# A decoder trunk on one core: the low parts of the down-projection weights made by accumulating DMA transfers

## The chip, the core and the metric

The kernel runs on 1 core of one Trainium2 chip. A time is the device time of one execution in microseconds. The time before is 1220.44 us, the median of 2 runs (1219.15 to 1221.73).

## What is computed

A two-layer decoder trunk on 256 tokens of width 1024 (float32, batch 1). Each layer adds to the residual h: half a SwiGLU feed-forward, a mixer (a state-space group beside a differential attention group, joined by one output projection), a cross attention into 256 memory tokens, and half a second SwiGLU. A final RMS norm follows.

```python
def swiglu(x, w_gate, w_up, w_down):
    return (jax.nn.silu(x @ w_gate) * (x @ w_up)) @ w_down
...
for l in range(DEPTH):                      # DEPTH = 2, D_MODEL = 1024, D_FF = 2816
    h = h + 0.5 * swiglu(rms_norm(h, ffn1_norm[l]), ffn1_w_gate[l], ffn1_w_up[l], ffn1_w_down[l])
    h = h + hybrid_mixer(rms_norm(h, mix_norm[l]), ...)
    h = h + memory_cross_attention(rms_norm(h, xattn_norm[l]), rms_norm(mem, mem_norm[l]), ...)
    h = h + 0.5 * swiglu(rms_norm(h, ffn2_norm[l]), ffn2_w_gate[l], ffn2_w_up[l], ffn2_w_down[l])
return rms_norm(h, final_norm)
```

There are four feed-forwards, and so four down projections of 2816 x 1024.

## The kernel before, in words

**Split products.** A matrix product is made of three products in the type float32r. Each operand is split into a high part, its copy in float32r, and a low part, what is left of it. The product is high x high + high x low + low x high. In the profile a weight's parts are called whi and wlo, an activation's xh and xl (or gT, oT, yT for both parts).

**The weight stream.** All weights lie in memory as 384 units of 128 x 1024 numbers (512 KB), in the order of their use (`stream_plan`, line 72). A unit is loaded by SyncE into one of 4 raw buffers (`load_to`, lines 450 to 453; N_RAW, line 33) and split in two halves of 512 columns into one of 5 pairs of hi and lo buffers (`split_unit`, line 457; N_W, line 34). ScalarE copies raw to hi, VectorE subtracts hi from raw into lo (`split`, line 408). For weights that follow a norm, the gain is multiplied in by both. A unit costs TensorE 12 matmuls of 512 columns, since there are two token tiles of 128, two halves and three products.

**Feed-forward** (`ffn`, line 707). 11 chunks of 256 hidden columns each take 4 units of the gate and up weights. ScalarE's silu (tile sg) and VectorE's product with the up half (tile g) follow, then transposes into gT. Two chunks behind, 2 units of the down projection are accumulated for each chunk (`mm_b`, line 513). So a steady period holds 6 units: 4 of gate and up, 2 of down. After the last chunk the last 4 down units remain. `blocks` (line 616) runs them all over the first token tile and then all over the second, so that the tail work of the first tile can begin early. During that first pass a new unit is wanted after only 6 matmuls. Each feed-forward has 22 down units, 18 in nine pairs and 4 in the tail.

**What sets the order.** The program is laid out in Python, instruction by instruction, by an estimated clock (`Clock`, line 122). Chains such as silu and transposes, the norm statistics, or the tables of the state-space model are tasks that are given out between the products of the main stream. Each engine then works through its own list in that order, and semaphores hold it wherever its data aren't there. Before each group of three products `tick` (line 493) calls `feed` (line 431), which gives out every half unit that is due: one wanted at most LEAD = 4.0 estimated us after the present place of the main stream, and only if its buffers are among the next 5 units. Units are given out strictly in order, so a down unit comes after the gate and up units ahead of it. `unit` (line 479) forces the unit that is wanted now.

**Buffers.** A raw buffer is loaded anew when all readers of it are done: ScalarE's copy and VectorE's subtraction of both halves. A hi or lo buffer is written anew when TensorE is done with the unit five before.

**Lines in the profile.** Helpers record every operation of an engine at one line: VectorE L223, ScalarE L257, GpSimd L280, matmuls L296, transposes L307, weight loads of the stream L453.

Of the kernel before, what the change touches and what calls it, by code (L numbers as in the profile page):

```python
# [11 lines left out]
F32 = mybir.dt.float32  # L12
# [3 lines left out]
AF = mybir.ActivationFunctionType  # L16
ALU = mybir.AluOpType
# [16 lines left out]
N_W = 5  # L34
N_S4 = 12
N_T5 = 3
LEAD = 4.0
STEP = 1.28
MARGIN = 0.2
BURST = 0.8  # L40
# [29 lines left out]


def stream_plan():
    """units of the weight stream in the order of use: (matrix, layer, index, kind, gain, units taken tile by tile)"""
    plan = []
    for l in range(L):
        def ffn(nm):
            for j in range(NCH):
                for kp in range(4):
                    plan.append((nm + "_gu", l, 4 * j + kp, "A", (nm, l, 2 * kp), 4 if j == 0 and len(plan) >= 4 else 1))
                if j >= LAG:  # L80
                    for f in range(2):
                        plan.append((nm + "_dn", l, 2 * (j - LAG) + f, "B", None, 1))
            for n in range(2 * (NCH - LAG), 2 * NCH):
                plan.append((nm + "_dn", l, n, "B", None, 2 * LAG))

        def chunk(nm, c, norm, skew):
            for kp in range(4):
                plan.append((nm, l, 4 * c + kp, "A", (norm, l, 2 * kp), skew))

        ffn("ffn1")  # L90
        for c in range(4):
            chunk("w_in", c, "mix", 4 if c == 0 else 1)
        for c in range(3):
            chunk("wkv", c, "mem", 1)
        for k in range(4):
            plan.append(("w_glu", l, k, "B", None, 4))
        for k in (4, 5, 6, 7, 0, 1, 2, 3):
            plan.append(("w_out", l, k, "B", ("ssm", l, k) if k < 4 else ("sub", l, 0), 4))
        for c in range(2):
            chunk("wq", c, "xattn", 4 if c == 0 else 1)  # L100
        chunk("wkv", 3, "mem", 1)
        for k in range(8):
            plan.append(("wo", l, k, "B", None, 4))
        ffn("ffn2")
    need, at, i = [], 0.0, 0
    while i < len(plan):
        n = plan[i][5]
        need += [at + STEP * k for k in range(n)]
        at += 2 * STEP * n
        i += n  # L110
    return plan, need


class Task:
    """a chain of instructions that is emitted piece by piece between the products of the main stream"""

    def __init__(self, gen, now):
        self.gen, self.t, self.done, self.waiters = gen, now, False, []
# [1 line left out]


class Clock:
    """Orders the emission: an estimate of when each engine gets to what it has been given."""

    def __init__(self, nc):
        self.nc = nc
# [38 lines left out]

    @contextmanager
    def aside(self):
        """what is given out here does not hold up the chain"""
        t = self.cur.t
        yield  # L170
        self.cur.t = t
# [11 lines left out]
                self.resume(x)  # L183

    def step_idle(self):
        """nothing to give the tensor engine: on to the next chain"""
        wake, _, x = heapq.heappop(self.heap)
        self.now = max(self.now, wake)
        self.resume(x)
# [122 lines left out]
class Trunk:  # L312
# [29 lines left out]
        self.mmfree = [0.0, 0.0]  # L342
        self.tpfree, self.tpown = [0.0, 0.0], {}

# [1 line left out]
    def s4t(self, shape, dt=F32, name="s4"):  # L346
        return self.s4.tile(shape, dt, tag="s4", name=name)

# [13 lines left out]
        self.tpfree[self.tpown.pop(id(p))[1]] = self.c.cur.t  # L362

    def tp_wait(self):
        """inside a task: until a bank for transposes is free"""
        while self.tpfree[-2] + TPW > self.c.now:
            yield max(self.c.now + 0.01, min(self.tpfree[-2] + TPW, self.c.now + 0.3))

# [20 lines left out]
        self.mmfree.append(self.c.cur.t)  # L389

    def acc_wait(self):
        """inside a task: until an accumulator is free"""
        while self.nacc >= 2 or self.accfree[0] + ACCW > self.c.now:
            yield self.c.now + 0.25 if self.nacc >= 2 else self.accfree[0] + ACCW

# [5 lines left out]
    def xt(self):  # L401
        return [self.xp.tile([128, 8, 128], F32R, tag=k, name=k) for k in ("xh", "xl")]

# [1 line left out]
    def copy(self, out, in_, scale=1.0):  # L405
        self.a.activation(out, in_, AF.Copy, scale=scale)

# [16 lines left out]
        return p  # L424

    def fork(self, *gens):
        """run chains side by side inside a task"""
        return [self.c.spawn(g, self.c.cur.t) for g in gens]

# [1 line left out]
    def feed(self, least=-1):  # L431
        """give out the halves of the units that are due, at least those of unit `least`"""
        c = self.c
        prev, c.cur = c.cur, self.stream
        n = len(self.plan)
        while self.nsplit < 2 * n:
            u, q = divmod(self.nsplit, 2)
            if u >= self.nfree + N_W or (u > least and self.need[u] + q * STEP / 2 > self.main + LEAD):
                break
            self.split_next()  # L440
        c.cur = prev
# [15 lines left out]
    def split_unit(self, i, q):  # L457
        kind, gain = self.plan[i][3:5]
        if q == 0:
            hi = self.hip.tile([128, 1024], F32R, tag="hi", name="whi")  # L460
            lo = self.lop.tile([128, 1024], F32R, tag="lo", name="wlo")
            self.w[i] = [hi, lo, 0.0, 0.0]
        hi, lo = self.w[i][:2]
        s = slice(512 * q, 512 * q + 512)
        r = self.raw[i]
        self.stream.t = 0.0
        if gain is None:
            self.split(hi[:, s], lo[:, s], r[:, s])
        else:
            nm, l, k = gain  # L470
            g = l * NGAIN + GOFF[nm] + k + (q if kind == "A" else 0)
            gc = self.gains[:, g:g + 1]
            self.a.activation(hi[:, s], r[:, s], AF.Copy, scale=gc)
            self.v.scalar_tensor_tensor(lo[:, s], r[:, s], gc, hi[:, s].bitcast(F32), op0=ALU.mult, op1=ALU.subtract)
        self.w[i][2 + q] = self.stream.t
        if q == 1:
            del self.raw[i]
# [11 lines left out]
    def free_unit(self):  # L489
        self.nfree += 1  # L490

# [1 line left out]
    def tick(self, ready):  # L493
        self.feed()
        self.c.run_due()
# [23 lines left out]
                self.p.matmul(acc[n], a, b[:, s], start=first and p == 0, stop=last and p == 2)  # L519

    def project(self, name, x, evac, preps=None):
        """a chunk of 512 columns for both token tiles; evac(t, psum) is the chain that follows"""
        self.c.run_due()
        ps = [self.mmt(), self.mmt()]
        out = []
        if preps is not None:
            us = []
            for t in range(2):
                self.c.wait(preps[t])
                for k in range(4):  # L530
                    if t == 0:
                        us.append(self.unit(name))
                    self.mm_a(ps[t], x[t], us[k], 2 * k, k == 0, k == 3)
                    if t == 1:
                        self.free_unit()
                out.append(self.c.spawn(evac(t, ps[t])))
        else:
            for k in range(4):
                u = self.unit(name)
                for t in range(2):  # L540
                    self.mm_a(ps[t], x[t], u, 2 * k, k == 0, k == 3)
                    if k == 3:
                        out.append(self.c.spawn(evac(t, ps[t])))
                self.free_unit()
        self.c.run_due()
        return out

    def opening(self, evac):
        """the first chunk, while x and the weights are still on their way in"""
        c = self.c  # L550
        c.now = c.busy["act"] = c.busy["dve"] = 3.9
        ps = [self.mmt(), self.mmt()]
# [53 lines left out]
        out = []  # L606
# [7 lines left out]
        return out  # L614

    def blocks(self, name, accs, xs, n, first, last, tail=None):
        """n units over token tile 0, then over tile 1; xs(t, k) is the stationary pair"""
        us = []
        out = []
        end = self.upos + n == len(self.plan)  # L620
# [9 lines left out]
                out.append(self.c.spawn(tail(t, accs[t])))  # L630
        return out

# [1 line left out]
    def prep(self, t, acc, coef):  # L634
        h = self.h[t]
        t0 = []
# [66 lines left out]
        return  # L703
        yield

# [1 line left out]
    def ffn(self, nm, preps, tail):  # L707
        bank = {}
        gT = {}
# [54 lines left out]
        base = NCH - LAG  # L764
        return self.blocks(nm + "_dn", accs, lambda t, k: xs(base + k // 2, k % 2, t), 2 * LAG, False, True, tail)

# [1 line left out]
    def exp_acc(self, out, x, n):  # L768
        v = self.v
        k, r, q = (self.sp1.tile([128, n], F32, tag=f"e{i}{n}", name="ex") for i in "krq")  # L770
# [20 lines left out]
        self.v.tensor_scalar(out, out, -MAGIC, None, op0=ALU.add)  # L791
        yield

# [1 line left out]
    def ssm_tables(self, l, tb):  # L795
        v, a, g, io = self.v, self.a, self.g, self.io
        t16 = lambda nm: self.sp1.tile([128, 16], F32, tag="p_" + nm, name=nm)
# [177 lines left out]
                g.dma_start(tt[r0:r0 + 16, :, j:4, :], ks[64 * e:64 * e + 16, :, 0:4 - j, :])  # L975
            yield

# [1 line left out]
    def mixer(self, l, preps, tb, tables, tail):  # L979
        v, c = self.v, self.c  # L980
        vt = w = cs = dtt = None
# [112 lines left out]
        def ssm_out(states):  # L1094
# [29 lines left out]
            for pb in range(2):  # L1124
                yield from self.tp_wait()
                p = self.transpose4(ygf, [256 * i + 128 * pb for i in range(4)])
                # columns of p are (i, gh, c): channel block 2*gh+pb, token 4*c+i
                pv = p.rearrange("p (i g c) -> p i g c", i=4, g=2)
                o = [x.rearrange("p (g b) (c i) -> p b i g c", b=2, i=4)[:, pb] for x in yt]
                self.split(o[0], o[1], pv)  # L1130
                self.tp_done(p)
# [156 lines left out]
        c.wait(*go)  # L1288
        return self.blocks("w_out", accs, lambda t, k: (mx[t][0][:, k, :], mx[t][1][:, k, :]), 4, False, True, tail)

# [1 line left out]
    def val_evac(self, ch, tag, after):  # L1292
        def f(t, ps):
            for x in after:
# [119 lines left out]
                    self.free_unit()  # L1414
        return self.blocks("wo", accs, lambda t, k: xs(t, 4 + k), 4, False, True, tail)

# [1 line left out]
    def setup(self):  # L1418
        nc, io, c = self.tc.nc, self.io, self.const
        g = self.g  # L1420
# [131 lines left out]


def lay_out(a):
    """host side: permutations, repeats and joins of the inputs"""
    f = {k: np.asarray(v) for k, v in a.items()}

    def type_a(w):
# [53 lines left out]
```

## Time and profile before

| | |
|---|---|
| median of 2 runs | 1220.44 us |
| span of the profiled execution, first to last instruction | 1217.4 us |
| TensorE's granted clock | 0.999 |
| VectorE, subtractions raw - hi without a gain (wlo<-raw,whi) | 224, mean 686 ns |
| ScalarE, copies raw to hi without a gain (whi<-raw) | 224, mean 624 ns |
| weight loads from memory on SyncE's queue | 382 of 512 KB, median 4.2 us to landing |
| read from memory | 207.06 MB |

Of the 224 halves without a gain 176 belong to the down projections (88 units); the other 48 are those of the gated linear unit and of the cross attention's output. The own time of the profiled execution is not listed apart from its span; the two runs of the table lie 1.8 to 4.3 us above that span. In the group lines the name left of the arrow is what is written, the names right of it are what is read; after the count stand the busy time, the mean of one in ns, and the idle time of the engine just before such instructions with what ended it. In a timeline a row gives the start, the time taken, engine, line and operation, and how many were merged. A stretch's row gives the length, then busy time and count for TensorE, its weight loads, VectorE, ScalarE and GpSimd, then the granted clock, the DMA engines' busy share and GB/s.

### The profile page before, as it was taken

What the parts mean: (1) busy time and instruction counts of PE and PEld (TensorE: products, weight loads), DVE (VectorE), ACT (ScalarE), POOL (GpSimd) and SP (SyncE); (2) the same over time, 40 slices, a digit from 0 to 9 for tenths busy, and PEclk for the clock granted to TensorE, in tenths of its full rate; (3) what the DMA queues carried; (4) which work ended last, traced back from release to release, by engine and by line L of the source; (5) the groups of instructions that cost most, each with busy time, mean ns of one, the idle gap of its engine ahead of it and who ended that gap; (6) DMA issues with size and microseconds to landing.
All of it is one profiled execution on the core that took longest, in us unless ns stands there. A gap on an engine that the chain in (4) does not pass through costs nothing.

```text
span 1217.4 us, 17907 instructions
## 1 busy us (share of the span) xinstructions
PE 1202.3 (99%) x6622; PEld 979.5 (80%) x6622; DVE 833.0 (68%) x1505; ACT 702.7 (58%) x1277; POOL 48.9 (4%) x111
## 2 busy tenths in 40 slices
PE   9999999999999999999999999999999999999997
PEld 7878888777888888888888888887678888888886
DVE  5787776498866678777666555565978675655664
ACT  6664545557857565644565544555686665644553
POOL 2110001000100010000100000000000000000000
PEclk9999999999999999999999999999999999999999
DMA  8566556534544466645656555655446445555652
GB/s 288 184 189 211 158 171 184 174 121 139 188 159 139 143 200 189 193 150 183 174 183 203 169 182 191 207 164 149 137 126 206 153 139 173 186 192 192 207 175 85
DMA packets 60439, 211.76 MB, mean 174 GB/s; under 512 B 7301, under 2 KB 8677, under 8 KB 60352
## 3 DMA queue, kind: packets, MB, share of 16 engines
q1 hardware_dynamic: 56448, 203.06, 52.6%
q0 software_dynamic: 2320, 6.08, 1.7%
q10 hardware_dynamic: 1584, 1.49, 0.4%
q8 instruction: 52, 0.85, 0.3%
q14 instruction: 35, 0.29, 0.1%
HBM read 207.06 MB, written 1.84 MB: 172 GB/s over the span
## 4 chain that ended last, share of the span: by engine, by line
PE 93%; DVE 2%; DMA 1%; ACT 1%; issue 1%; ACTq 0%; POOLq 0%; POOL 0%; DVEq 0%
PE mm L296 54%; PE acc L296 32%; PE tp L307 5%; PE tp L296 2%; DMA uq<-z 1%; DVE wlo L223 1%; DVE p L223 1%; ACT whi L257 0%; DVE nm L223 0%; DMA h<-in_x 0%; ACT z L257 0%; ACT junk L257 0%; ACT up L257 0%; ACTq L266 0%; DVE sb L223 0%
## 5 line engine op out<-in xcount | busy, mean ns | idle before, releaser
L223 DVE SCALAR_TENSOR_TENSOR wlo<-raw,gains,whi 128x512 fp32r<-128x512 f32 x544 | 383.4, 746 | 96.1 <-ACT whi L257 91.8
L257 ACT ACTIVATE whi<-raw,gains 128x512 fp32r<-128x512 f32 x544 | 353.4, 713 | 14.2 <-DMA raw<-in_wst 6.8
L296 PE MATMUL mm<-whi,xh 128*128 128x512 f32 x896 | 357.0, 398 | 0.0
L296 PE MATMUL mm<-whi,xl 128*128 128x512 f32 x896 | 349.8, 390 | 0.0
L296 PE MATMUL mm<-wlo,xh 128*128 128x512 f32 x896 | 349.5, 390 | 0.3 <-DVE wlo L223 0.3
L296 PE MATMUL acc<-whi,gT 128*128 128x512 f32 x704 | 240.0, 402 | 0.0
L296 PEld LDWEIGHTS mm<-whi,xh 128*128 128x128 f32 x896 | 168.5, 188 | 37.4 <-issue 2.4
L296 PEld LDWEIGHTS mm<-whi,xl 128*128 128x128 f32 x896 | 168.5, 188 | 35.8
L296 PEld LDWEIGHTS mm<-wlo,xh 128*128 128x128 f32 x896 | 168.8, 188 | 32.8 <-DVE wlo L223 0.6
L223 DVE TENSOR_TENSOR wlo<-raw,whi 128x512 fp32r<-128x512 f32 x224 | 147.3, 686 | 36.1 <-ACT whi L257 34.4
L257 ACT ACTIVATE whi<-raw 128x512 fp32r<-128x512 f32 x224 | 130.6, 624 | 62.2 <-DMA raw<-in_wst 41.0
L257 ACT ACTIVATE sg<-mm,rstd 128x256 f32<-128x256 f32 x88 | 41.8, 475 | 194.7 <-PE mm L296 194.5
L296 PEld LDWEIGHTS acc<-whi,gT 128*128 128x128 f32 x704 | 132.2, 188 | 26.8 <-issue 1.1
L296 PE MATMUL acc<-wlo,gT 128*128 128x512 f32 x352 | 137.4, 390 | 0.0
L223 DVE SCALAR_TENSOR_TENSOR g<-mm,rstd,sg 128x256 f32<-128x256 f32 x88 | 42.4, 482 | 127.1 <-ACT sg L257 126.5
L296 PE MATMUL mm<-whi,mem 128*128 128x512 f32 x256 | 92.6, 410 | 0.0
L296 PEld LDWEIGHTS acc<-wlo,gT 128*128 128x128 f32 x352 | 66.4, 189 | 11.0
L257 ACT ACTIVATE xh<-tp 128x512 fp32r<-128x512 f32 x40 | 23.9, 598 | 76.9 <-PE tp L307 76.9
L296 PEld LDWEIGHTS mm<-whi,mem 128*128 128x128 f32 x256 | 48.1, 188 | 11.5 <-issue 1.3
L296 PE MATMUL mm<-wlo,mem 128*128 128x512 f32 x128 | 50.9, 398 | 3.5 <-DVE wlo L223 3.5
L223 DVE TENSOR_TENSOR xl<-tp,xh 128x512 fp32r<-128x512 f32 x40 | 27.5, 687 | 31.4 <-ACT xh L257 31.4
L223 DVE TENSOR_TENSOR gT<-tp,gT 128x512 fp32r<-128x512 f32 x44 | 30.4, 691 | 26.7 <-ACT gT L257 26.6
(218 smaller groups left out, 1099.8 us busy)
## 6 DMA issues: line engine op xcount, KB each, us to landing
raw<-in_wst SPq DMA_DIRECT2D x382, 512.0 KB, 4.2
h<-in_x SPq DMA_DIRECT2D x4, 256.0 KB, 5.3
raw<-in_wst SPq DMA_DIRECT2D x4, 256.0 KB, 5.3
mem<-in_mem POOLq DMA_DIRECT2D x2, 512.0 KB, 6.7
uq<-z ACTq DMA_DIRECT2D x8, 128.0 KB, 4.7
bglu<-in_b_glu POOLq DMA_DIRECT2D x2, 512.0 KB, 4.0
scr<-sk POOLq DMA_DIRECT2D x4, 192.0 KB, 3.4
out_h<-fo SPq DMA_DIRECT2D x2, 320.0 KB, 2.3
```

Source lines behind the costliest of these rows:

```text
L223: r = getattr(self.e, name)(*a, **k)
L257: r = self.e.activation(out, in_, func, **k)
L296: r = self.e.matmul(out, lhsT, rhs, **k)
L307: r = self.e.transpose(out, in_, ident)
```

## The change

Units of the down projections (names that end in `_dn`) are split in another way. ScalarE copies raw to hi as before, and then copies hi, negated, to lo. After the second half one DMA transfer issued by GpSimd adds the whole unit of weights onto lo, 128 x 1024 numbers, so that lo holds weights minus hi. For units of odd number its source is the raw buffer, for those of even number the weights in memory once more. Both halves count as ready, in the estimated clock, when this transfer is. `feed` gives such units out up to DMA_LEAD = 3.0 us earlier. VectorE no longer takes part in these units.

```diff
 LEAD = 4.0
+DMA_LEAD = 3.0
...
-            if u >= self.nfree + N_W or (u > least and self.need[u] + q * STEP / 2 > self.main + LEAD):
+            early = DMA_LEAD if self.plan[u][0].endswith("_dn") else 0.0
+            if u >= self.nfree + N_W or (u > least and self.need[u] + q * STEP / 2 > self.main + LEAD + early):
                 break
...
-        if gain is None:
+        if self.plan[i][0].endswith("_dn"):
+            self.a.activation(hi[:, s], r[:, s], AF.Copy)
+            self.a.activation(lo[:, s], hi[:, s].bitcast(F32), AF.Copy, scale=-1.0)
+            if q == 1:
+                self.g.dma_start(lo, r if i % 2 else self.io["wst"][i], accum_op=ALU.add)
+                self.w[i][2] = self.stream.t
+        elif gain is None:
             self.split(hi[:, s], lo[:, s], r[:, s])
```

The rest of the diff takes out comments and docstrings.

## The prediction

> **What bounds the kernel now.** I read first the page's busy times and its chain of waits, then the table of who waited for whom, then busy times by stretch. The four stretches are the steady parts of the four feed-forwards, in order; the fifth is one period of six weight units.
>
> ```profile
> span 1217.4 us, 17907 instructions
> PE 1202.3 (99%) x6622; PEld 979.5 (80%) x6622; DVE 833.0 (68%) x1505; ACT 702.7 (58%) x1277; POOL 48.9 (4%) x111
> PE 93%; DVE 2%; DMA 1%; ACT 1%; issue 1%; ACTq 0%; POOLq 0%; POOL 0%; DVEq 0%
> ```
>
> ```profile
> PEld mm L296 <- DVE wlo L223: 6.7, 7, 1.8
> PE mm L296 <- DVE wlo L223: 3.8, 5, 1.4
> ...
> L296 PE MATMUL acc<-wlo,gT 128*128 128x512 f32 x352 | 137.4, 390 | 0.0
> L296 PE MATMUL mm<-wlo,mem 128*128 128x512 f32 x128 | 50.9, 398 | 3.5 <-DVE wlo L223 3.5
> ```
>
> ```profile
> 37.00:198.00 161.00, 161.00 (x936) 128.84 (x935) 125.20 (x296) 85.57 (x150) 12.95 (x25) 1.00 0.61 184
> 434.00:610.00 176.00, 176.00 (x1009) 143.40 (x1008) 131.74 (x288) 96.47 (x168) 8.83 (x18) 1.00 0.59 180
> 650.00:820.00 170.00, 170.00 (x776) 140.13 (x775) 99.82 (x155) 89.30 (x156) 1.49 (x4) 1.00 0.57 187
> 1040.00:1194.00 154.00, 154.00 (x698) 126.75 (x697) 89.36 (x139) 80.02 (x139) 0.00 (x0) 1.00 0.57 188
> ...
> 1160.00:1176.80 16.80, 16.80 (x77) 13.85 (x76) 9.73 (x16) 8.74 (x16) 0.00 (x0) 1.00 0.56 189
> ```
>
> TensorE is busy in every microsecond of all four feed-forwards, at a granted clock of 1.00. The matmuls that read a down projection's low part (acc<-wlo,gT) never stood idle: 0.0 us before 352 of them. What TensorE does wait on VectorE's low parts (3.8 and 6.7 us, which overlap) falls elsewhere: the idle row is that of the memory projections (mm<-wlo,mem), which the change leaves alone. So VectorE's work on the down projections costs nothing now, and taking it away can't make these stretches shorter. The question is only whether the new way delivers late.
>
> **The change, part by part.** Removed and added on the engines:
>
> ```profile
> L223 DVE TENSOR_TENSOR wlo<-raw,whi 128x512 fp32r<-128x512 f32 x224 | 147.3, 686 | 36.1 <-ACT whi L257 34.4
> L257 ACT ACTIVATE whi<-raw 128x512 fp32r<-128x512 f32 x224 | 130.6, 624 | 62.2 <-DMA raw<-in_wst 41.0
> ...
> L280 POOL DMA_DIRECT2D mem<-in_mem x2 | 1.2, 594 | 0.0
> ```
>
> There are 4 x 22 = 88 down units of two halves. VectorE loses 176 subtractions of 686 ns, 121 us: worth 0, as shown. ScalarE gains 176 copies; with no such row I price them as its plain half copies, 624 ns: 110 us. In one period that is 4 x 0.62 = 2.5 us on top of 8.74 of 16.80, so ScalarE still has 5.6 us over, and the cost by volume is 0. Without that cover it would be 2.5 us in each of 36 periods, 90 us. GpSimd issues 88 transfers, at about 0.6 us each (the mem row) 53 us on an engine busy for 48.9; what queues behind a waiting issue there is the two-step rstd, of which a feed-forward needs two, ahead of its first unit. I take 0 for that. Even units read their weights a second time from memory, 44 x 0.524 = 23 MB beside 203 MB.
>
> What does count is latency. The low part was ready one VectorE instruction after the high part. Now it is ready after four ScalarE copies and a whole 512 KB accumulating transfer, issued only after the second half. Call d the time from the last copy to the landing. No accumulate is in the trace; the nearest rows are plain transfers:
>
> ```profile
> raw<-in_wst SPq DMA_DIRECT2D x382, 512.0 KB, 4.2
> mem<-in_mem POOLq DMA_DIRECT2D x2, 512.0 KB, 6.7
> bglu<-in_b_glu POOLq DMA_DIRECT2D x2, 512.0 KB, 4.0
> scr<-sk POOLq DMA_DIRECT2D x4, 192.0 KB, 3.4
> bias<-scr POOLq DMA_DIRECT2D x1, 512.0 KB, 5.3
> fn<-in_final_norm POOLq DMA_DIRECT2D x1, 512.0 KB, 5.1
> ```
>
> GpSimd's 512 KB transfers land in 4.0 to 6.7 us. One pass of a unit through the 16 engines takes 0.56 x 16.80 / 6 = 1.6 us. An accumulate must read its target as well as its source. Low end: the second reading is free, d = 0.6 + 4.0 = 4.6. High end: the slowest row and a whole extra pass, d = 0.6 + 6.7 + 1.6, rounded to 9.0. I take the middle, 6.8, because loads of weights run beside it in every period, as beside the slow mem row.
>
> The Trainium skill bears on the second reading (Collectives: The Full Stack, "Part 3: Why 7× under link rate — side-by-side accounting"): an add in the DMA engine needs two source reads on one ring, and a reduce there came out at half the rate of a copy (measured ratio 1.93). By it a unit's accumulate would take an estimated 1.93 x 1.6 = 3.0 us of all engines; without it 1.6, and d would stand about 1.5 us apart between the two. No accumulate in this trace tells which.
>
> Now the time that is there. The code gives down units out up to 3 us earlier, so that the second unit's second half no longer stands behind a silu; but transfers can't start before the weights, slots and ScalarE allow. A steady pair of down units in the last feed-forward:
>
> ```profile
> 1150.63 1.15 ACT L257 ACTIVATE whi<-raw 128x512 fp32r<-128x512 f32 x2 [0.95 <-DMA raw<-in_wst]
> 1152.50 0.63 ACT L257 ACTIVATE whi<-raw 128x512 fp32r<-128x512 f32 x1 [0.72 <-DMA raw<-in_wst]
> ...
> 1160.03 0.40 PE L296 MATMUL acc<-wlo,gT 128*128 128x512 f32 x1
> ...
> 1163.02 0.39 PE L296 MATMUL acc<-wlo,gT 128*128 128x512 f32 x1
> ```
>
> First unit: 1150.63 + 2.5 = 1153.1, wanted at 1160.03: 6.9 us for the transfer. Second: copies end at 1155.6, wanted at 1163.02: 7.4. With d = 6.8 nothing is late; with 9.0 it is 2.1 a pair.
>
> In the first layer's feed-forwards (936 and 1009 TensorE instructions of the first two stretches against 776 and 698 of the others: the state-space tables are made between the products) some pairs have less:
>
> ```profile
> 187.40 1.66 ACT L257 ACTIVATE whi<-raw 128x512 fp32r<-128x512 f32 x3
> ...
> 195.06 0.40 PE L296 MATMUL acc<-wlo,gT 128*128 128x512 f32 x1
> ...
> 584.10 1.66 ACT L257 ACTIVATE whi<-raw 128x512 fp32r<-128x512 f32 x3
> ...
> 589.59 0.39 PE L296 MATMUL acc<-wlo,gT 128*128 128x512 f32 x1
> ```
>
> These leave 195.06 - 189.9 = 5.2 and 589.59 - 586.6 = 3.0 us, 4.1 in the mean. I choose 9 of the 36 pairs as such, half of those of that layer. With d = 6.8 each is 2.7 late: 24 us.
>
> The four tails are the worst place. There the last four down units are run over one token tile first, so that a unit is wanted each 1.36 us, while ScalarE now needs 2.5 for one:
>
> ```profile
> 1184.25 1.15 ACT L257 ACTIVATE whi<-raw 128x512 fp32r<-128x512 f32 x2 [0.94 <-DMA raw<-in_wst]
> ...
> 1193.41 0.48 ACT L257 ACTIVATE sg<-mm,rstd 128x256 f32<-128x256 f32 x1 [0.37 <-PE mm L296]
> ...
> 1195.25 0.60 ACT L257 ACTIVATE gT<-tp 128x512 fp32r<-128x512 f32 x1 [0.84 <-PE tp L307]
> 1195.74 3.74 ACT L257 ACTIVATE whi<-raw 128x512 fp32r<-128x512 f32 x7
> ...
> 1203.45 0.39 PE L296 MATMUL acc<-wlo,gT 128*128 128x512 f32 x1
> ```
>
> After the second sg (1193.9) stand half of the second tail unit (1.25), gT (to 1195.9), its other half (to 1197.1) and the third (to 1199.6). The fourth also needs its raw buffer: it is that of the second unit before the tail, which an accumulate now reads until it lands. That unit's copies end at 1184.25 + 2 x 2.5 = 1189.25, it lands at 1196.05, and the new load (4.2) at 1200.25. So the fourth is copied by 1202.75 and lands at 1209.55, where it was wanted at 1203.45: 6.1 late, four times, 24 us.
>
> Sum with d = 6.8: 0 + 24 + 24 = 48 us. The profiled execution's span is 1217.4 us; the runs' median, 1220.44, has 3.0 more around it, which I leave as it is: 1220.4 + 48 = 1268.5 us. With d = 4.6: 0 + 9 x 0.5 + 4 x 3.25 (ScalarE alone holds the tail, 1199.6 + 2.5 + 4.6 against 1203.45) = 17.5, 1238 us. With d = 9.0: 27 x 2.1 + 9 x 4.9 + 4 x 10.5 = 143, 1363 us.
>
> **The rivals.** *The lead covers it.* If the second reading rides along and the landing is like scr's 3.4, d is 4.0: no pair is late, and a tail only by 1199.6 + 2.5 + 4.0 - 1203.45 = 2.65. That is 11 us, 1231 us, not to be told from no change. It decides wherever d is below 5.1 (9 x 1.0 + 4 x 3.75 = 24 us, 2%). For it: bglu's 4.0 and the 7 us of a steady pair. Against: mem's 6.7, fn and bias above 5. The Trainium skill's fit for transfers issued by GpSimd (DMA: Bandwidth & Descriptors, "Anatomy of one DMA") gives an estimated 2.0 + 524 KB / 436 = 3.2 us for a plain one; every 512 KB row here is above it.
>
> *The DMA engines become the bound.* A period's loads take 0.56 x 16.80 = 9.4 us of them. Two accumulates fit as long as each takes under (16.80 - 9.4) / 2 = 3.7 us, 2.3 passes. At four passes, 6.4 us each, a period lasts 22.2, 5.4 more: 36 x 5.4 = 194, and a tail's four accumulates with four loads 32 us against some 17, 4 x 15 = 60: 1475 us. For it: the traffic is already 0.57 to 0.61. Against: no row here shows so slow a transfer.
>
> *The relief helps.* If the waits on low parts went, TensorE would gain at most 6.7 us, 1214 us. Against: they aren't where down units are split, and the accumulate is no shortcut even if all goes as meant.
>
> **How the numbers follow.** Late by a few microseconds in tails and short pairs (1268.5): 0.48. Covered (1231): 0.29. DMA-bound, or d at 9 and above: 0.21. Relief: 0.02, half of it over 2%. A measurement of this kernel can tell about 2% from no change. The range, 1227 to 1365, runs from a little under the covered case to d = 9.0 and leaves out most of the DMA-bound one. Slower by over 2%: 0.48 + 0.21 and little of the rest, 0.69; within 2%: 0.30; faster: 0.01.
>
> **What would show it.** VectorE's wlo<-raw,whi falls from x224 to x48; ScalarE shows x176 copies of whi into wlo near 620 ns; GpSimd 44 + 44 transfers into wlo. Right: these land in 5 to 7 us after issue, TensorE's acc<-wlo,gT has some 48 us of idle time that a DMA into wlo ended, half of it in four places, and the second layer's steady pairs show none. Wrong: that idle time lies evenly over all 36 pairs, or the DMA share nears 1 in the periods (then the engines are the bound), or TensorE stays busy through the tails (then the lead covers it).

## The result, and the profile after

The changed kernel takes 1364.34 us (median of 2 runs, 1364.12 to 1364.57) where the kernel before takes 1220.44: a ratio of 1.119, 95% interval 1.117 to 1.121, 144 us slower. Forecast were 48 us. The page of the changed kernel, first its span, busy times and chain, then groups:

```profile
span 1362.3 us, 18270 instructions
PE 1250.9 (92%) x6622; PEld 1004.4 (74%) x6622; DVE 725.6 (53%) x1329; ACT 813.3 (60%) x1453; POOL 125.5 (9%) x199
PE 57%; DMA 22%; issue 13%; ACT 4%; DVE 4%; ACTq 0%; POOLq 0%; POOL 0%; DVEq 0%; SPq 0%
...
L297 PE MATMUL acc<-whi,gT 128*128 128x512 f32 x704 | 263.7, 438 | 0.5 <-ACT gT L258 0.5
L297 PE MATMUL acc<-wlo,gT 128*128 128x512 f32 x352 | 155.6, 442 | 96.0 <-DMA wlo<-in_wst 65.9
...
L258 ACT ACTIVATE wlo<-whi 128x512 fp32r<-128x512 f32 x176 | 111.4, 633 | 5.6
...
L281 POOL DMA_DIRECT2D wlo<-in_wst x44 | 38.4, 874 | 575.8 <-ACT wlo L258 428.7
```

Two things lengthened the span by 144.9 us. TensorE idles 1362.3 - 1250.9 = 111.4 us where it idled 15.1, 96.3 more, and 96.0 of idle time stands before the products with a down unit's low part, the row that had 0.0. And TensorE is busy for 1250.9 us with the same 6622 instructions that took 1202.3, 48.6 more: the two acc rows above rose from 402 and 390 ns a product to 438 and 442. The DMA rows:

```profile
q1 hardware_dynamic: 56448, 203.06, 46.8%
q0 software_dynamic: 14992, 52.22, 20.0%
...
raw<-in_wst SPq DMA_DIRECT2D x382, 512.0 KB, 4.5
wlo<-in_wst POOLq DMA_DIRECT2D x44, 512.0 KB, 7.7
wlo<-raw POOLq DMA_DIRECT2D x44, 512.0 KB, 7.7
```

An accumulate lands 7.7 us after its issue, from either source. GpSimd begins to issue 0.29 us after the last copy's end (median over the 72 units of the pairs), so the forecast's d is 8.0, not 6.8. A steady pair, in TensorE's timeline:

```profile
1232.67 0.48 PE L297 MATMUL acc<-whi,gT 128*128 128x512 f32 x1
1234.43 0.47 PE L297 MATMUL acc<-wlo,gT 128*128 128x512 f32 x1 [1.28 <-DMA wlo<-in_wst]
```

Nearly every pair waits, 33 of the 36, not only the short ones: the first low part of a pair is used, at the median, 0.13 us after its landing. From the first down unit to the start of the tail the second layer's feed-forwards last 20.5 and 19.2 us longer than before, the first layer's 28.2 and 33.0. The tails are 11.2, 9.3, 13.6 and 10.4 longer. That is 101 us in the pairs and 45 in the tails. Of these, 66 and 30 are idle time before low parts; the rest is the busier TensorE.

The last tail shows the second loss. After the long wait the products stand 0.42 us apart, and then 0.23 again; the stretches' rows give the granted clock (the column after GpSimd's):

```profile
1341.25 0.63 PE L297 MATMUL acc<-whi,gT 128*128 128x512 f32 x2
1345.75 0.79 PE L297 MATMUL acc<-wlo,gT 128*128 128x512 f32 x1 [3.88 <-DMA wlo<-raw]
1346.35 1.05 PE L297 MATMUL acc<-whi,gT 128*128 128x512 f32 x2
1347.20 0.63 PE L297 MATMUL acc<-wlo,gT 128*128 128x512 f32 x1
...
1352.44 0.39 PE L297 MATMUL acc<-wlo,gT 128*128 128x512 f32 x1
1352.68 0.62 PE L297 MATMUL acc<-whi,gT 128*128 128x512 f32 x2
1353.13 0.39 PE L297 MATMUL acc<-wlo,gT 128*128 128x512 f32 x1
```

```profile
1345.70:1351.20 5.50, 5.45 (x13) 4.29 (x14) 3.04 (x8) 1.93 (x7) 0.57 (x1) 0.51 0.01 1
1351.20:1354.80 3.60, 3.60 (x18) 2.87 (x16) 1.39 (x2) 1.88 (x4) 0.00 (x0) 1.00 0.38 146
```

The trace has 22 stretches at half clock, 99 us in sum, the last 6.5 behind the last product. In them 124 products stand 0.42 us or more behind the one before instead of 0.227. If each of TensorE's instructions is set against the mean of its kind in the trace of before, 40 of the 48.6 us fall in these stretches and 7 on the first product behind a wait at full clock. The trace of before has such a stretch only at its very end.

### The profile page after: what moved, and what is told of

Same layout as the page of the kernel before. It is cut to its first block, busy times and chain, and to the rows that moved or that the text cites. A ratio compares the mean times of both kernels' runs of the same rounds, so it can differ in the third digit from the quotient of the medians.

```text
span 1362.3 us, 18270 instructions
## 1 busy us (share of the span) xinstructions
PE 1250.9 (92%) x6622; PEld 1004.4 (74%) x6622; DVE 725.6 (53%) x1329; ACT 813.3 (60%) x1453; POOL 125.5 (9%) x199
## 4 chain that ended last, share of the span: by engine, by line
PE 57%; DMA 22%; issue 13%; ACT 4%; DVE 4%; ACTq 0%; POOLq 0%; POOL 0%; DVEq 0%; SPq 0%
PE acc L297 26%; PE mm L297 26%; DMA wlo<-in_wst 14%; PE tp L308 4%; DMA wlo<-raw 4%; DMA raw<-in_wst 3%; DVE wlo L224 2%; ACT whi L258 2%; PE tp L297 1%; DMA uq<-z 1%; ACT wlo L258 1%; DVE p L224 1%; ACT junk L258 0%; ACT gT L258 0%; ACT z L258 0%
## 5 line engine op out<-in xcount | busy, mean ns | idle before, releaser
L297 PE MATMUL acc<-whi,gT 128*128 128x512 f32 x704 | 263.7, 438 | 0.5 <-ACT gT L258 0.5
L297 PE MATMUL acc<-wlo,gT 128*128 128x512 f32 x352 | 155.6, 442 | 96.0 <-DMA wlo<-in_wst 65.9
L258 ACT ACTIVATE whi<-raw 128x512 fp32r<-128x512 f32 x224 | 136.5, 622 | 57.4 <-DMA raw<-in_wst 44.5
L297 PEld LDWEIGHTS acc<-whi,gT 128*128 128x128 f32 x704 | 147.7, 210 | 30.7 <-ACT gT L258 1.0
L297 PEld LDWEIGHTS acc<-wlo,gT 128*128 128x128 f32 x352 | 74.0, 210 | 124.6 <-issue 56.5
L258 ACT ACTIVATE wlo<-whi 128x512 fp32r<-128x512 f32 x176 | 111.4, 633 | 5.6
L281 POOL DMA_DIRECT2D wlo<-in_wst x44 | 38.4, 874 | 575.8 <-ACT wlo L258 428.7
L258 ACT ACTIVATE gT<-tp 128x512 fp32r<-128x512 f32 x44 | 26.2, 596 | 104.8 <-PE tp L308 104.6
L258 ACT ACTIVATE xh<-tp 128x512 fp32r<-128x512 f32 x40 | 23.9, 598 | 96.3 <-PE tp L308 96.3
```

The costliest lines, as they stand in the source:

```text
L258: r = self.e.activation(out, in_, func, **k)
L281: r = f(out, *a, **k)
L297: r = self.e.matmul(out, lhsT, rhs, **k)
```

## The experiments

Theory A: the accumulate lands too late for the time that the stream leaves. Rivals: ScalarE's extra copies (S), and the DMA engines' throughput (B). Unless a range is given, a time is that of one run beside one of the kernel before (1219 to 1220 us; seven of them, with a median of 1219.5, for `mem_hold`, `raw_pairs` and `raw_pairs_hi_first`). A diff is against the changed kernel; for `late_split` and `solo` against the kernel before.

**act_only.** ScalarE's copies without the transfer:

```diff
-            if q == 1:
-                self.g.dma_start(lo, r if i % 2 else self.io["wst"][i], accum_op=ALU.add)
-                self.w[i][2] = self.stream.t
+            self.v.tensor_tensor(lo[:, s], r[:, s], lo[:, s].bitcast(F32), op=ALU.add)
```

> The changed kernel, but VectorE adds the raw weights onto the negated high part that ScalarE writes; no accumulating transfer. Theory A (the transfer's latency: 8.0 us from the last copy to the landing, and a raw buffer held until then): ScalarE's 176 extra copies cost nothing, 1215 to 1232 us, TensorE's acc<-wlo,gT idle under 5 us. Rival S (ScalarE's 111 us of extra copies make the low parts late): over 1290 us, with most of the 96 us of idle time still there.

Measured 1222.71 us, TensorE busy 1202.1 us. ScalarE's 111 us lie beside other work, as forecast, and the tails last as long as before. S falls.

**plain_copy.** The transfer without the add, so that the low part holds the weights themselves:

```diff
-                self.g.dma_start(lo, r if i % 2 else self.io["wst"][i], accum_op=ALU.add)
+                self.g.dma_start(lo, r if i % 2 else self.io["wst"][i])
```

> The changed kernel with the same 88 transfers of 512 KB by GpSimd, but without the add: the low part then holds the weights themselves, so this part of the computation is changed. If the second reading makes the transfer slow (rival B: engine time, 2.9 us of all 16 engines each against 1.6 for a load), the landing falls from 7.7 to about 6 us and the time to 1250 to 1290. If it is the way of issuing that is slow, the landing stays above 7 us and the time above 1330.

Measured 1262.93 us.

```profile
q0 software_dynamic: 14992, 52.22, 12.1%
...
wlo<-in_wst POOLq DMA_DIRECT2D x44, 512.0 KB, 5.7
wlo<-raw POOLq DMA_DIRECT2D x44, 512.0 KB, 4.4
```

With the same bytes by the queue's count, the add costs 101 us. Take from each q0 share the 1.7% of 1217.4 us that this queue had before: a plain transfer holds all 16 engines for (152.6 - 20.7) / 88 = 1.50 us, an accumulate for (272.5 - 20.7) / 88 = 2.86 us. The ratio is 1.9. The Trainium skill's half rate for an add (Collectives: The Full Stack, "Part 3: Why 7× under link rate — side-by-side accounting") agrees.

**solo.** Transfers behind the end of the kernel, one after the other. All but three wait for the landing of the one before; those three, the accumulates from a buffer into a float32 target, run beside the plain transfer from memory ahead of them. `r` is a buffer, `lo` the target:

```diff
+        for m in range(3):
+            self.g.dma_start(lo, r, accum_op=ALU.add)
+            self.g.dma_start(lo, self.io["wst"][1], accum_op=ALU.add)
+            self.g.dma_start(lo, r)
+            self.g.dma_start(lo, self.io["wst"][2])
...
```

> The kernel before, with 24 transfers of 512 KB by GpSimd added behind its end, one after the other with nothing beside them: accumulates and plain ones, from a buffer and from memory, into float32r and into float32; it adds time at the end and changes nothing else. If latency is mostly the transfer's own, an accumulate lands alone in 5.5 to 7 us and a plain one in 3.5 to 4.5; if the 7.7 us are mostly contention with the loads, an accumulate alone lands within 1 us of a plain one, under 4.8. The source makes under 0.5 us of difference.

GpSimd's timeline, in the order of the diff:

```profile
1220.34 0.95 POOL L280 DMA_DIRECT2D slo<-sraw  x1 [6.74 <-ACT slo L257]
1225.21 0.87 POOL L280 DMA_DIRECT2D slo<-in_wst  x1 [3.92 <-DMA slo<-sraw]
1231.05 0.56 POOL L280 DMA_DIRECT2D slo<-sraw  x1 [4.96 <-DMA slo<-in_wst]
1234.27 0.54 POOL L280 DMA_DIRECT2D slo<-in_wst  x1 [2.67 <-DMA slo<-sraw]
```

From issue to issue 4.9 us for the accumulate from a buffer, 5.8 from memory, 3.2 for the plain one from a buffer. To the landing alone it is 4.5 to 4.6, 5.4 to 5.5, 2.9, and for a plain one from memory 3.9 (into a float32 target; the plain ones from memory that had an accumulate issued right behind them took 4.1 to 4.3). So neither expectation holds quite: alone an accumulate is some 1.6 us slower than a plain transfer, the source makes 0.9, and of the 7.7 us in the kernel 2.2 to 3.2 are from what runs beside it. (Into a float32 target the accumulate from memory took 5.5 to 5.6.)

**all_mem.** Every accumulate reads memory, to break a loop through the raw buffers:

```diff
-                self.g.dma_start(lo, r if i % 2 else self.io["wst"][i], accum_op=ALU.add)
+                self.g.dma_start(lo, self.io["wst"][i], accum_op=ALU.add)
```

> The changed kernel, but every accumulate reads the weights from memory once more; no raw buffer is held by one. Theory A in its sharper form (a loop: the second down unit's accumulate frees its raw buffer only when it lands, the load of the last gate and up unit waits for that, and behind it on the same queue the loads of the next pair, so a period lasts 18.4 us where TensorE needs 16.8): steady periods of the second layer fall to at most 17.3 us, the time to 1275 to 1315. Rival B (the DMA engines' load of 0.78 sets the time): the same traffic or a little more, 1355 to 1380.

Measured 1362.96 us. My sharper form of A fell: nothing is won by freeing the raw buffers early. The landings rose to 9.1 us. The time lies in B's range; `all_raw` below decides on B.

**small_loads.** A quarter of the gate and up loads:

```diff
+            part = 256 if self.plan[self.nload][0].endswith("_gu") and self.nload > 8 else 1024
+            self.tc.nc.sync.dma_start(r[:, 0:part], self.io["wst"][self.nload][:, 0:part])
...
+                rs = r[:, 0:256].unsqueeze(1).to_broadcast([128, 2, 256])
```

> The changed kernel, but from the ninth unit on only the first quarter of each gate and up unit is loaded, and this quarter stands in for the others in the split, so these products are changed; all engines have the same work and the accumulates are as they were. Theory: the accumulate lands late (7.7 us from issue, where alone it took 4.5 from a buffer and 5.5 from memory) because it shares the DMA engines with the loads. Then the landing falls to 5 to 6.3 us and the time to 1225 to 1265, with steady pairs of the second layer on time. If the landing is set by GpSimd's issuing or by the two accumulates of a pair overlapping, it stays above 7 us and the time above 1320.

Measured 1269.13 us, landings 5.8 and 5.7 us; the pairs of the second layer last 142.7 and 142.4 us where before had 140.3 and 140.4. What runs beside an accumulate delays it. The time missed its range by 4 us, because the tails stayed long (17 to 25 us).

**all_raw.** The other way round:

```diff
-                self.g.dma_start(lo, r if i % 2 else self.io["wst"][i], accum_op=ALU.add)
+                self.g.dma_start(lo, r, accum_op=ALU.add)
```

> The changed kernel, but every accumulate reads the raw buffer; each raw buffer of a down unit is held until the landing. If the source matters as in the lone transfers (4.5 us from a buffer, 5.5 from memory), the landing of the first of a pair falls by some 0.5 to 1 us and the time to 1325 to 1355. If holding the buffers matters more, 1365 to 1400.

Measured 1287.52 us: 77 us gone by one word, more than either expectation. The landing's median is 5.4. An accumulate holds the engines as long as ever (21.0% of 1285.7 us in the first row below, 2.83 us each), so the throughput of the engines is not what cost the 77 us: B falls. Why does it land earlier? The DMA rows by queue, for the changed kernel from an accumulate's issue to the next, and for all_raw from issue to landing:

```profile
q0 software_dynamic: 14992, 52.22, 21.0%
```

```profile
DMA packets 218, 0.81 MB, mean 324 GB/s; under 512 B 20, under 2 KB 20, under 8 KB 218
...
q1 hardware_dynamic: 215, 0.80, 97.9%
q0 software_dynamic: 3, 0.01, 9.0%
...
wlo<-in_wst POOLq DMA_DIRECT2D x1, 512.0 KB, 7.5
```

```profile
q0 software_dynamic: 161, 0.59, 68.1%
q1 hardware_dynamic: 55, 0.17, 9.0%
...
wlo<-raw POOLq DMA_DIRECT2D x2, 512.0 KB, 4.9
```

In the changed kernel (1245.5 to 1248 us) the engines are full of weight loads, 97.9%, and of the accumulate there are 3 packets. Most of it moves only when the loads are done; by then its pair's second accumulate is there too, and the two share the engines for the next 6 us. In all_raw (1161 to 1165.6 us) the loads are 9%. The pairs shown are no exceptions: over the 44 accumulates of even units, the loads hold 0.87 of the engines in the 2.5 us behind the issue in the changed kernel and 0.42 in all_raw (medians). An even unit that reads memory frees its raw buffer as soon as it is copied, and the load of the unit four later in the stream goes ahead of the accumulate that is wanted now: in the changed kernel's pair it was issued at 1244.59 us, as the copy ended, and landed at 1250.53. Reading the raw buffer holds that load back: in all_raw's pair it was issued at 1165.70, when the accumulate had landed.

**mem_hold** tests this. Almost all from memory, but the buffer is held:

```diff
-                self.g.dma_start(lo, r if i % 2 else self.io["wst"][i], accum_op=ALU.add)
+                self.g.dma_start(lo[:, 0:960], self.io["wst"][i][:, 0:960], accum_op=ALU.add)
+                self.g.dma_start(lo[:, 960:1024], r[:, 960:1024], accum_op=ALU.add)
```

> The changed kernel, but each accumulate is two: columns 0 to 959 read memory, for units of either parity, and columns 960 to 1023 read the raw buffer, which so is held until the second one lands. Queue theory (what made the landing 7.7 us is that raw buffers that were free early let loads of later units queue on the DMA engines ahead of the accumulate; reading the raw buffer holds those loads back): close to the kernel in which all read the raw buffer (1287.5), at most 25 us above it for the second issue and the smaller rows, 1285 to 1315, the large transfers landing in 5 to 6.5 us. Source theory (reading memory itself is what is slow beside loads): close to the kernel in which all read memory (1363.0), over 1340.

Measured 1312.67 us: 50 of the 75 us between all_mem and all_raw came back by the holding, with 64 of the 1024 columns read from the buffer. It reads more from memory than the changed kernel, which took 52 us longer. The landings of 7.0 us are longer than I expected. What the other 25 us are (the second issue, the memory as a source) was not told apart.

**late_split.** Idle time without any accumulate:

```diff
-            if u >= self.nfree + N_W or (u > least and self.need[u] + q * STEP / 2 > self.main + LEAD):
+            if u >= self.nfree + N_W or (u > least and self.need[u] + q * STEP / 2 > self.main + LEAD - (4.5 if self.plan[u][0].endswith("_dn") and self.plan[u][5] == 1 and u % 2 == 0 else 0.0)):
...
+                for _ in range(2):
+                    self.v.tensor_tensor(lo[:, s], r[:, s], hi[:, s].bitcast(F32), op=ALU.subtract)
```

> The kernel before, no accumulate in it, but the first down unit of each of the 36 pairs is split only when it is wanted, and VectorE does its first subtraction three times over; so TensorE must wait some 3 us in each pair for VectorE. Clock theory (an idle gap of TensorE of about 2 us or more is followed by a stretch at half the granted clock, whatever made the gap): half-clock stretches in most of the 36 periods, TensorE's busy time up from 1202 to 1240 or more, the mean clock under 0.975, and the time some 110 us of idle plus 40 to 60 us above before, 1350 to 1400. Rival (the transfers themselves slow TensorE, by their reads and writes): the clock stays above 0.995 and TensorE's busy time at 1202, whatever the idle time.

Measured 1303.54 us, mean clock 0.987, TensorE busy for 1226.9 us: all three miss their ranges, since the waits were shorter than I had reckoned, most of them 1.4 us, and these left the clock alone. The rival's clock above 0.995 and busy time of 1202 us are missed too. Where a wait reached some 1.9 us, the half clock mostly came (not behind one of 1.99 us at 552.8 and one of 2.71 at 115.4):

```profile
512.44 0.50 PE L296 MATMUL acc<-wlo,gT 128*128 128x512 f32 x1 [1.92 <-DVE wlo L223]
...
513.68 1.05 PE L296 MATMUL acc<-whi,gT 128*128 128x512 f32 x2
514.53 0.63 PE L296 MATMUL acc<-wlo,gT 128*128 128x512 f32 x1
...
517.34 0.63 PE L296 MATMUL acc<-whi,gT 128*128 128x512 f32 x2
```

```profile
513.30:516.60 3.30, 3.30 (x9) 2.48 (x8) 3.21 (x6) 0.00 (x0) 0.00 (x0) 0.50 0.64 196
```

Seven such stretches inside the span, with no accumulate in the program. So the half clock comes without the transfers, behind idle time; and `raw_pairs_hi_first` below has 72 accumulates, hardly any waits and no such stretch before its end.

**hi_first** and **hi_first_all.** Products with high parts first, by unit, and by pair and in the tails (there two loops, one over the part, stand round the products):

```diff
-                    for t in range(2):
-                        self.mm_b(accs[t], *xs(i, f, t), u, i == 0 and f == 0, False)
+                    for part in range(2):
+                        for t in range(2):
+                            self.mm_p(accs[t], *xs(i, f, t), u, i == 0 and f == 0, False, part)
```

> The changed kernel with the 12 products of each down unit in pairs in another order: the 8 that read the high part first, then the 4 that read the low part, so that the low part is wanted 1.6 us later; tails as they were. Window theory (what counts is the 8.0 us from the last copy to the landing against the time that is left): 1.4 to 1.6 us less idle time in nearly every one of 36 pairs, 96 falls to 40 to 55, half-clock stretches from 22 to 8 to 14, the time to 1270 to 1305. Rival B (the DMA engines' throughput sets the period): the period stays 18.4 us in the second layer, the time above 1340.

> The changed kernel, but in each pair the 16 products with high parts of both down units come first and the 8 with low parts after them, and in a tail's first pass likewise for all four units. The first low part is wanted 3.4 us later than in the changed kernel, the tail's last one not later. With only the order by unit the time was 1307.7. Window theory: steady pairs on time (140 to 143 us for the nine periods of a second-layer feed-forward, from 149 to 150), the tails shorter by 2 to 4 us each, 1255 to 1285. Loop theory (any delay comes back through buffers and in-order engines): no more than 10 us below 1307.7.

Measured 1307.67 and 1303.51 us. Later use of the low parts helps, by 57 us for 1.6 us in each pair, and then no more: the pairs of the second layer still last 145 to 150 us. B would have kept the first of these times above 1340. The loop theory was right about the size of the second step; that raw buffers and the engines' own order hand a landing's delay on to the next pair is argued, not shown.

**halves.** An accumulate for each half:

```diff
-            if q == 1:
-                self.g.dma_start(lo, r if i % 2 else self.io["wst"][i], accum_op=ALU.add)
-                self.w[i][2] = self.stream.t
+            self.g.dma_start(lo[:, s], r[:, s] if i % 2 else self.io["wst"][i][:, s], accum_op=ALU.add)
```

> The changed kernel with two accumulates of 256 KB for each down unit, each issued behind its own half's copies, so the first starts 1.2 us earlier and moves half as much. Window theory: the first half, on which TensorE waits first, lands in about 5.5 us after its copy instead of 8.0, and 2 to 3.7 us earlier in all; idle time falls from 96 to under 55, the time to 1265 to 1315. Rival B: as many bytes and more transfers, 1350 to 1380.

Measured 1333.36 us, 18 us above the range of the window theory and 17 below B's, and half the bytes landed after 7.9 us: what the transfer waits for does not shrink with it.

**raw5.** N_RAW = 5 and N_S4 = 11:

> The changed kernel with five raw buffers instead of four, paid for with one of the twelve shared work buffers. Loads can start one unit earlier. If the copies of the first down unit of a pair stand waiting for its load, as the profile has it, they start 1.3 to 2.5 us earlier and the time falls to 1290 to 1335; if the hi and lo buffers hold them, less than 10 us changes. The work buffer taken away may cost a few microseconds outside the feed-forwards.

Measured 1325.32 us. ScalarE's idle time before plain copies falls from 57.4 to 18.9 us, so loads that start earlier help the copies, though the landings stay at 7.8 and 8.1.

**tails_only, raw_pairs, raw_pairs_hi_first.** The accumulate in the tails alone, then in the pairs alone from raw buffers, then this with high parts first by pair:

```diff
-        if self.plan[i][0].endswith("_dn"):
+        if self.plan[i][0].endswith("_dn") and self.plan[i][5] > 1:
```

> The changed kernel with the accumulate in the 16 units of the four tails alone; the 72 units of the pairs are split by VectorE as before. If the tails cost what the changed kernel's tails lasted longer (from 11.8 us each to 23.0, 21.1 and 25.4, and the last 10.4 more), and the pairs are a cost of their own: 1255 to 1270. If the tails are only late because the pairs before them hold buffers and ScalarE: under 1245.

> The changed kernel with all accumulates from the raw buffer, in the 72 units of the pairs alone; the 16 units of the tails are split by VectorE as before. The tails of the kernel with all from the raw buffer lasted 45 us longer than before in sum; if they are a cost of their own, 1235 to 1250, what is left being the short windows of the first layer. If the accumulates of the pairs pass a delay on: over 1255.

> The same as the run with raw buffers in pairs alone, and the 16 products with high parts of a pair come before the 8 with low parts. Window theory: the first layer's short pairs get 3.4 us more, so nearly nothing is late: 1218 to 1230, the same as before within the measurement, and not faster, since TensorE was never waiting for these low parts. If the accumulates cost TensorE time in another way, 1235 or more.

Measured 1253.59 us for the tails alone, 34 to 35 above before and 1.4 under the range. The pairs alone: 1247.44 us (4 runs, 1245.69 to 1248.04; ratio 1.022, interval 1.021 to 1.024). With high parts first: 1228.00 us (4 runs; ratio 1.007, interval 1.005 to 1.009), and TensorE is busy as before:

```profile
PE 1203.3 (98%) x6622; PEld 977.5 (80%) x6622; DVE 747.4 (61%) x1361; ACT 796.4 (65%) x1421; POOL 111.1 (9%) x183
```

So the way back from 1364 has four steps: 77 us for the source (by `mem_hold` some 50 of them for the held buffer), 40 for the tails, 19 for low parts that were late in pairs, mostly of the first layer, 8 left. No version with accumulates beat the kernel before.

## Why the prediction was wrong

- *The removal is worth nothing, TensorE bounds the feed-forwards*: right. VectorE fell from 833.0 to 725.6 us busy and nothing was gained; with 72 of 88 units moved and everything else mended the time is still 0.7% above before.
- *ScalarE's copies cost nothing by volume*: right (act_only; 111.4 us against 110).
- *GpSimd's issue at 0.6 us*: it took 0.87 us. It is in the landing's time and changes little.
- *"I take the middle, 6.8"*: this step failed first. d was 8.0. Put into the forecast's own working, 8.0 gives 27 x 1.1 + 9 x 3.9 = 65 us in pairs and 4 x 8.5 = 34 in tails, 99 us of idle time; measured were 96, 66 in the pairs and 30 in the tails. By layer it fits less well: 45 and 20 us in the pairs of the first and second layer by the working, 38.6 and 27.5 measured. plain_copy bears the working out as well: d is 5.7 there, which gives 9 x 1.6 + 4 x 4.35 = 32 us of idle time, and 33 were measured. The 512 KB rows that the range came from were plain transfers; in the first 2.5 us behind their issue loads held from none to 0.62 of the engines, against 0.87 behind an even unit's accumulate. The rows that told were there: in the period of the steady pair shown in the prediction, whose copies run at 1150.6 to 1153, the loads come in a bunch.

```profile
1148.00:1156.00 8.00, 8.00 (x37) 6.62 (x36) 4.75 (x8) 3.46 (x6) 0.00 (x0) 1.00 0.86 309
1157.00:1161.00 4.00, 4.00 (x21) 3.24 (x20) 1.76 (x4) 2.08 (x4) 0.00 (x0) 1.00 0.00 0
```

  The DMA share, last but one, is 0.86 around the copies and 0.00 soon after, so the mean of 0.56 says little about what an accumulate meets. And the sum gave nothing for raw buffers that come free early, where they let the bunch go first.
- *The sum held idle time alone*: the second failure. It has no term for a TensorE that runs slower after waiting. TensorE's busy time rose by 48.6 us, 40 of them in half-clock stretches. The sum for d = 9.0, 1363 us, hits the measured time by luck: it held 143 us of idle time, where there were 96 of it and 49 of a slower TensorE.
- *Half of the idle time in four tails, none in steady pairs*: wrong with d. The tails cost 45 us (24 forecast), the pairs 101 (24 forecast), and the prediction's own sign of being wrong came: idle time in nearly all 36 pairs. plain_copy, with landings of 4.4 and 5.7 us, spreads as I had drawn it: 2.5 us longer in the second layer's pairs, 22 in the first's, 21 in the tails.
- *The DMA engines become the bound*: not in that form. An accumulate holds them for 2.86 us, under the 3.7 at which a period's work would no longer fit, and all_raw and changed kernel differ by 77 us with the same work for them. What an accumulate meets on the engines cost time, and how long it holds them itself (plain_copy, with half of that, is 101 us shorter), but not the engines' work in sum.

## What to carry to other kernels

A transfer that is put on the path of a busy stream must be priced with what is queued ahead of it on the DMA engines when it is issued, not by its lone or median landing; look at which loads a freed buffer lets go first. Where a bound engine would wait, price the wait and the slower clock behind it. And work taken from an engine is worth nothing where the bound engine never waits for it (its idle time before the products that read the result is 0.0), however many microseconds that work takes.

## What I had not expected of the hardware

- Gaps of TensorE of about 2 us were enough for a stretch of 3.4 us, or a multiple, at half clock: in the changed kernel gaps of 1.88, 1.97 and 2.01 us have one behind them, while one of 2.38 us (before 1216.07) has none; gaps of 1.4 us never had one. The Trainium skill's rule of thumb, no idle gaps above 3.4 us (TensorE: Matmul & The Clock Gate, "HAM oscillation — how this bites in real kernels"), is too generous here. It is the idle time in a fixed window that tells: the changed kernel's 22 stretches all begin on one grid of 3.413 us. Of its grid windows at full clock, each with 1.96 us or more of idle TensorE has a half-clock stretch behind it and none with less than 1.87; the gap of 2.38 us straddles two windows, with 0.87 and 1.52. In all_raw the bounds are 1.96 and 1.82. One stretch of late_split, at 69.5 us, doesn't fit: its window held 1.1 us.
- The source of an accumulate changed its landing by 0.9 us alone; in the stream the choice of source moved the whole kernel by 77 us, most of it through a buffer.
- Accumulates of 256 KB landed no earlier (7.9 us) than those of 512 KB (7.7).
